# Recurrences of an RWKV-7 layer: solving a batch ahead of need, with a copy of the keys reloaded when it is turned

## The chip, the cores and the metric

One core of one Trainium2 chip runs the whole program in one launch. The metric is device microseconds of that core, as the median of several executions; lower is better. A core has five engines that each work through their own instructions in order and meet through semaphores: PE (matmuls and transposes by matmul; its weight loads are shown as PEld), DVE, ACT and POOL (elementwise work), and SP, which issues the DMAs.

## The reference, cut to what matters

Two layers of a backbone over 1024 latent and 256 context tokens, width 1024, in float32. Layer 0 is attention with a gated recurrence and an expert mixture. Layer 1, where the change lies, is a bidirectional RWKV-7 mixing followed by an expert mixture. For each of 16 heads of 64 channels, in both directions, the mixing runs this recurrence over the context and then over the latent tokens:

```python
def step(s, inp):
    w_t, k_t, v_t, a_t, b_t = inp[:5]
    sa = jnp.einsum('bhvk,bhk->bhv', s, a_t)
    s = s * w_t[:, :, None, :] + sa[..., None] * b_t[:, :, None, :] + v_t[..., None] * k_t[:, :, None, :]
    y = jnp.einsum('bhvk,bhk->bhv', s, inp[5]) if r is not None else None
    return s, y
```

Afterwards the outputs of both directions are added, normalised by head, given a bonus, gated and multiplied by an output matrix (`rw_wo`), and the expert mixture and a final norm follow.

## The kernel before

The program runs in stages: layer 0, the projections of layer 1 (`Proj1`, which writes the images of queries, keys and values to DRAM as `iAR`, `iBK`, `iV`), the recurrences (`Wkv.run`, here 2296 to 2938 us of the profile), the output projection (`mix_out1`, 2825 to 3028 us, overlapping the end of the recurrences) and the experts of layer 1 (`moe`, from 3035 us).

The recurrence is cut in chunks of 64 tokens (`C`). A chunk is one step of matmuls with a state of 64x64 for each head, once the inverse of a unit triangular 64x64 matrix of that chunk is known. A *group* holds one chunk of four heads-and-directions on each half of the 128 partitions. There are 4 sets of heads (`pg`) and 20 chunks, so 80 groups and 80 steps. Eight groups make a *batch*; there are 10 batches, and their inverses are computed together, since each has 32 matrices. In the order of steps two sets of heads alternate, so that one set's state update has about one step of slack.

What happens to a group, with the names of the code:
- `images` loads keys (`bk`, one load for two groups: L1941 to L1943) and queries (`ar`, L1952), multiplies them (PE, into tile `G`, L1960), copies the triangles into the batch's tile `lab` (ACT, L1962 and L1964) and masks the rest (DVE, L1970).
- `turn` transposes the group's keys (PE, tile `T`, L1980) and copies them to `bkt` (ACT, L1981).
- `solve` has two parts. The first transposes `lab` into `lp` (DVE, L2010), clears `rp` (POOL) and does 31 rounds of a multiply and a subtract (L2018 and L2019), on DVE for the first batch and on POOL for all later ones. The second transposes `rp` back into `db` and `dtb` (DVE, L2022 and L2023) and copies a quarter of it (ACT, L2026). `db` is the same memory as `lp`.
- `join`, called for each half of a batch, builds the 64x64 inverses out of two 32x32 ones by matmuls (L2039 and L2047) and ACT copies (L2042 and L2049). It reads `db`.
- `values` loads and turns the values of two groups (tile `vt`, L1990; PE L1993; ACT L1999 and L2000).
- `step` multiplies query images with the state (`XS`, L2064; ACT copy `xs`, L2066), then by the inverse (L2072, ACT L2074), gives the new state (L2078; DVE `st`, L2084 and L2086; ACT L2089) and the output (`Y`, L2069 and L2094; ACT `ys`, L2099; a store at L2109).

`run` prepares 16 groups and the first batch's inverses, and then issues the steps. Step `at` (from 0) also turns the group 15 ahead, makes the images 16 ahead, and, at fixed places of a batch, runs the parts of `solve` and `join` for the *next* batch: the first part of `solve` in the batch's step 0 (`at % 8 == 0`), after the last `join` of the running batch has read `db`; the second part in step 6, between the step's first matmuls and its multiplication by the inverse; `join` from step 7 to step 1 of the next batch.

On PE, ACT and DVE the instructions of the steps are issued in the order in which the code emits them (`manual_schedule`). That ends with step 66 (`FREE`); the rest, and the order on SP and POOL everywhere, is a planner's. Memory comes from rings: `NG` = 17 places for `ar` (five of them in memory named `early`, which the projections held before), `bkt` and `lrb`, two for `lab`, four pairs of groups for `bk` (`bks`, in `early`).

The output projection takes over the memory of the recurrences (class `Tail`): its weights `raws[0..3]` are loaded into `bs`, `bks[0]`, `bks[1]`, `bks[2]`, and the row that scales them (`row0`, L818) into `bks[3]`. Its first half treats the heads of the first two sets, tile by tile of 128 tokens, 8 tiles (product at L853); its second half the other heads (L902).

Of the kernel before, what the change touches and what calls it, by code (L numbers as in the profile page):

```python
# [1322 lines left out]
C = 64  # L1323
# [556 lines left out]
class Wkv:  # L1880
# [3 lines left out]
    NG = 17  # L1884
# [8 lines left out]
    def __init__(self, g, p, pp):  # L1893
        nc, A = g.nc, g.A
        self.g, self.p, self.pp = g, p, pp
        self.iAR = [g.dram(f"iAR{k}", [128, 20, 4, 2 * C]) for k in range(4)]
        self.iBK = [g.dram(f"iBK{k}", [128, 20, 4, 2 * C]) for k in range(4)]
        self.iV = [g.dram(f"iV{k}", [128, 10, 4, 2 * C]) for k in range(4)]
        self.mask = g.wmask
        self.ring = {}  # L1900
        self.st = {}
        self.at = {}

        a, b = (g.wkvp.tile([128, 5, 1024], F, name="early", tag=n) for n in ("mvh", "mvl"))
        self.bks, self.bs, self.ars = [a[:, k] for k in range(4)], a[:, 4], [b[:, k] for k in range(5)]
        self.nar = self.nbk = 0
        self.persist("dtb", [128, 32, C], 2)
# [14 lines left out]
    def new_batch(self, groups):  # L1922

        lab = self.p.tile([128, 32, C], F, name="lab", tag="lab", bufs=2)
        if len(groups) < 8:
            self.g.nc.gpsimd.memset(lab[:, 16:, :], 0.0)
        return dict(groups=groups, lab=lab, gr=[])

    def images(self, b):
# [6 lines left out]
        if k == 0:  # L1936
            b["bk"] = bk = self.bks[self.nbk % 4].rearrange("p (c u x) -> p c u x", c=2, u=4)
            self.nbk += 1
            src = self.iBK[pg][:, c:c + 2].rearrange("p c u t -> p (c u) t")
            dst = bk.rearrange("p c u t -> p (c u) t")  # L1940
            nc.sync.dma_start(dst[0:64], src[0:64])  # L1941
            nc.sync.dma_start(dst[64:128, :, C:], src[64:128, :, 0:C])
            nc.sync.dma_start(dst[64:128, :, 0:C], src[64:128, :, C:])  # L1943
# [27 lines left out]
        b["gr"].append(dict(pg=pg, c=c, ar=ar, lrb=lrb, lu=4 * n, bk=bk))  # L1971

    def turn(self, gr):

        g, nc, p, pp = self.g, self.g.nc, self.p, self.pp
        gr["bkt"] = bkt = p.tile([128, 4, 2 * C], F, name="bkt", tag="bkt", bufs=self.NG)
        tp = pp.tile([128, 4, 128], F, name="T", tag="T", bufs=self.NT)
        bk = gr.pop("bk")
        for u in range(4):
            nc.tensor.transpose(tp[:, u], bk[:, u], g.ident)  # L1980
        nc.scalar.copy(bkt, tp)  # L1981
# [20 lines left out]
    def solve(self, b, eng):  # L2002
# [18 lines left out]
        db = lp  # L2021
# [89 lines left out]
    def run(self):  # L2111
# [7 lines left out]
        made, turned, ys = 0, 0, {}  # L2119
# [10 lines left out]
        def turn():  # L2130
            nonlocal turned
            if turned < N:
                self.turn(bs[turned // 8]["gr"][turned % 8])
                turned += 1
# [5 lines left out]
        def pair():  # L2140
            for _ in range(2):
                images()
            turn()
            turn()
# [14 lines left out]
        while made < 16:  # L2159
            pair()  # L2160
        none = iter(())
        solve, joins, last = none, [none, none], none
        E = mybir.EngineType
        with ExitStack() as written:
            written.enter_context(g.tc.manual_schedule(engines={E.PE, E.Activation, E.DVE}))
            for at, (k, n) in enumerate(order):
# [17 lines left out]
                if at:  # L2184
                    turn()
                if at % 8 == 6:
                    run(solve)
# [12 lines left out]
                if at % 8 == 0:  # L2200
                    run(joins[1])
                    if more:
                        solve = self.solve(bs[k + 1], g.nc.gpsimd)
                        run(solve)
                images()
# [5 lines left out]
class Tail:  # L2211


    def __init__(self, w):
# [5 lines left out]

        def half(n, dt=R, tag="bkt", bufs=w.NG):
            return sum((get(tag, bufs, dt, 512) for _ in range(n)), [])
# [11 lines left out]
        a = halves(get("lab", 2, F, m=2)) + half(4, F) + halves(ar(3, F) + b[:1])  # L2234
        cs = half(4)
        mw = halves(get("lab", 2, R, m=2) + get("lp", 1, R) + get("rp", 1, R)) + half(4) + halves(ar(2, R))
# [149 lines left out]
```

## Time and profile before

| | us |
|---|---|
| median of 3 runs (3696.99 to 3702.59) | 3699.67 |
| the profiled execution | 3699.94 |
| its span, first to last instruction | 3698.2 |
| granted TensorE clock, mean of the span | 0.92 |

Over the span PE is busy for 3168.2 us (86%), DVE 2475.2 (67%), ACT 2199.7 (59%), POOL 1083.1 (29%). These shares are averages over stages with different limits; the change touches one stage of some 640 us and what follows it.

### The profile page before, as it was taken

The page shows a single profiled execution, that of the slowest core. Times are in us where ns is not written, and L with a number is a line of the kernel's source. Part 1 is how long each engine was busy: PE and PEld are TensorE (multiplying, and loading weights), DVE is VectorE, ACT ScalarE, POOL GpSimd, SP SyncE. Part 2 cuts the span into 40 slices and gives each one's busy share as a digit, 9 for nine tenths or more (in the row PEclk, how much of TensorE's full clock was granted, in tenths as well). Part 3 has the DMA queues.
Part 4 walks back from the last instruction along what each step waited for, and adds up shares of the span by engine and source line. Part 5 has one row for each costly group of instructions (what it writes and reads, how often), then busy time and mean ns, then how long its engine had stood idle before and what let it go on. Part 6 is the DMA issues. An engine that isn't in the chain of part 4 may idle for free. (4 is left out here: it accounts for less than half of the span.)

```text
span 3698.2 us, 68014 instructions
## 1 busy us (share of the span) xinstructions
PE 3168.2 (86%) x27017; PEld 2487.3 (67%) x27017; DVE 2475.2 (67%) x3341; ACT 2199.7 (59%) x3985; POOL 1083.1 (29%) x1195
## 2 busy tenths in 40 slices
PE   7997989599999999798888876676767876999998
PEld 5884677477777777567766765565655554887776
DVE  5666783666766766666985895433445457888888
ACT  4564573366666666335644663676666544878776
POOL 2213002301111111234653661555466221111111
PEclk9998999799999999898889987888788987999999
DMA  5117716468888887444862783343336559999995
GB/s 200 59 39 273 282 34 202 165 248 285 280 290 290 280 286 272 152 129 130 220 186 67 197 222 95 103 101 97 89 110 183 155 200 321 384 377 384 354 379 216
DMA packets 579366, 770.59 MB, mean 208 GB/s; under 512 B 106868, under 2 KB 371048, under 8 KB 572904
## 3 DMA queue, kind: packets, MB, share of 16 engines
q1 hardware_dynamic: 564104, 717.22, 57.8%
q0 software_dynamic: 14944, 49.03, 4.8%
q8 instruction: 212, 3.47, 0.4%
q14 instruction: 106, 0.87, 0.1%
HBM read 638.96 MB, written 127.18 MB: 207 GB/s over the span
## 5 line engine op out<-in xcount | busy, mean ns | idle before, releaser
L192 DVE TENSOR_TENSOR elo<-raw,ehi 128x2048 fp32r<-128x2048 f32 x378 | 859.4, 2289 | 296.6 <-ACT ehi L191 295.4
L191 ACT ACTIVATE ehi<-raw 128x2048 fp32r<-128x2048 f32 x384 | 734.9, 1916 | 214.0 <-PE h L1158 82.4
L1158 PE MATMUL h<-ehi,xhi 128*128 128x512 f32 x512 | 208.0, 406 | 0.0
L1158 PE MATMUL h<-elo,xhi 128*128 128x512 f32 x512 | 203.0, 396 | 0.0
L1158 PE MATMUL h<-ehi,xlo 128*128 128x512 f32 x512 | 202.8, 396 | 0.0
L2018 POOL TENSOR_TENSOR tmp<-lp,rp 128x31 f32<-128x31 f32 (+15 forms) x279 | 145.0, 520 | 169.6 <-DVE lp L2010 148.8
L1102 PE MATMUL h<-ehi,wx 128*128 128x512 f32 x512 | 163.3, 396 | 0.0
L2019 POOL TENSOR_TENSOR rp<-rp,tmp 128x31 f32<-128x31 f32 (+15 forms) x279 | 153.8, 551 | 21.5
L1477 PE MATMUL pj<-mvh,whi 128*128 128x384 f32 (+1 forms) x512 | 149.3, 326 | 2.6 <-ACT vv L1787 2.5
L1477 PE MATMUL pj<-mvl,whi 128*128 128x256 f32 (+1 forms) x512 | 146.5, 320 | 4.1 <-DVE mvl L192 3.8
L1477 PE MATMUL pj<-mvh,wlo 128*128 128x256 f32 (+1 forms) x512 | 148.6, 323 | 0.7 <-POOL wlo L192 0.7
L1122 POOL DMA_INDIRECT xg<-s_hl,idx x16 | 15.8, 987 | 451.1 <-PE tr L1137 446.7
L1265 PE MATMUL y<-ehi,wh 128*128 128x512 f32 x512 | 143.6, 397 | 2.3 <-DVE wh L192 2.3
L1970 DVE TENSOR_TENSOR ar<-G,wmask 64x512 f32<-64x512 f32 (+1 forms) x110 | 69.9, 635 | 112.5 <-PE G L1960 103.1
L2078 PE MATMUL XS<-sv,bkt 128*64 128x64 f32 x1216 | 59.4, 247 | 94.4 <-ACT sv L2074 93.5
L1080 ACT ACTIVATE xm<-tr,c_mcol 128x128 f32<-128x128 f32 x256 | 95.6, 453 | 60.9 <-PE tr L1069 36.5
L1087 POOL DMA_INDIRECT xg<-s_hl,idx x16 | 24.2, 1511 | 362.5 <-PE tr L1069 339.1
L2078 PEld LDWEIGHTS XS<-sv,bkt 128*64 128x64 f32 x1216 | 48.0, 154 | 109.5 <-ACT sv L2074 99.2
L1226 POOL DMA_INDIRECT s_xl<-ys,idx x16 | 52.4, 3274 | 230.7 <-DVE ys L1225 230.7
L216 PE MATMUL pj<-xhi,whi 128*128 128x512 f32 (+1 forms) x336 | 119.1, 355 | 0.0
L216 PE MATMUL pj<-xlo,whi 128*128 128x512 f32 (+1 forms) x336 | 119.0, 354 | 0.0
L216 PE MATMUL pj<-xhi,wlo 128*128 128x512 f32 (+1 forms) x336 | 118.8, 354 | 0.0
(562 smaller groups left out, 9328.0 us busy)
## 6 DMA issues: line engine op xcount, KB each, us to landing
raw<-in_exp_w SPq DMA_DIRECT2D x379, 1024.0 KB
modw<-in_mod_w SPq DMA_DIRECT2D x48, 1024.0 KB
wraw<-in_rw_rkv SPq DMA_DIRECT2D x48, 512.0 KB
s_iAR<-ar SPq DMA_DIRECT2D x32, 384.0 KB
s_iBK<-bk SPq DMA_DIRECT2D x32, 384.0 KB
ar<-s_iAR SPq DMA_DIRECT2D x88, 128.0 KB
early<-s_iBK SPq DMA_DIRECT2D x40, 256.0 KB
early<-s_iBK SPq DMA_DIRECT2D x80, 128.0 KB
```

The source lines that it names most:

```text
L191: nc.scalar.activation(hi, src, AF.Copy)
L192: (sub or nc.vector).tensor_tensor(lo, src, hi.bitcast(F), op=ALU.subtract)
L216: nc.tensor.matmul(ps[:m, :b - a], wt[:, k, :m], xt[:, k, a:b], start=k == 0 and n == 0, stop=k == kt - 1 and n == 2)
L1080: self.nc.scalar.activation(f[:, k], src[:, k], AF.Identity, scale=a, bias=b)
L1102: nc.tensor.matmul(hs[which], a[:, kk], b[:, k], start=kk == 0 and a is x[0] and b is w[1], stop=kk == 7 and a is x[1])
L1158: nc.tensor.matmul(hs[which], a[:, kk], b[:, k], start=kk == 0 and a is x[0] and b is w[1], stop=kk == 7 and a is x[1])
L1265: nc.tensor.matmul(y[:, 512 * n:512 * n + 512], a[:, kk % 4], b[:, k, 512 * n:512 * n + 512], start=kk == 0 and a is hh and b is hi, stop= ...
L1477: nc.tensor.matmul(ps[q], wk[:, k], xk[:, a:b], start=k == 0 and n == 0, stop=k == KT - 1 and n == 2)
L1970: nc.vector.tensor_tensor(o4, g4, self.mask[r, None, :, x].to_broadcast([r.stop - r.start, 2, 2, x.stop - x.start]), op=ALU.mult)
L2018: eng.tensor_tensor(t, lp[:, k + 1:, k:k + 1].to_broadcast([128, n, w]), rp[:, k:k + 1, 0:w].to_broadcast([128, n, w]), op=ALU.mult)
L2019: eng.tensor_tensor(rp[:, k + 1:, 0:w], rp[:, k + 1:, 0:w], t, op=ALU.subtract)
L2078: nc.tensor.matmul(S[R[h], u], bkt[:, u, V[h]], sv[:, u, V[h]], start=True, stop=True)
```

## The change

- The inverses of a batch are begun one batch earlier. `solve` for the second batch starts before step 0; in step 5 of each batch the second part of `solve` for the next batch is run, and right behind it the first part for the batch after that. Before, the two parts of one solve lay in step 0 and step 6 of the same batch.
- For this, `db` gets memory of its own (`bs`) instead of `lp`'s, `lab` has three places instead of two, and images are made 18 groups ahead (`LEAD`) with `NG` = 20 places for `ar` and `lrb`.
- Keys are turned two steps ahead instead of 15, and `bkt` has 5 places instead of 17. Since `bk` is not kept until then, `turn` loads the group's keys a second time, by three DMAs of its own (`load_bk`). Of the four places of `bks`, two now serve the images (a pair of groups each) and two the turns (four groups in all).
- `Tail`, which reuses the memory, takes half-size tiles from `ar` instead of `bkt`, and `lab` in threes.

```diff
--- before.py
+++ after.py
@@ -1881,7 +1881,8 @@
 
 
 
-    NG = 17
+    NG = 20
+    LEAD = 18
     NYS = 2
     NSV = 5
     NT = 2
@@ -1903,7 +1904,7 @@
 
         a, b = (g.wkvp.tile([128, 5, 1024], F, name="early", tag=n) for n in ("mvh", "mvl"))
         self.bks, self.bs, self.ars = [a[:, k] for k in range(4)], a[:, 4], [b[:, k] for k in range(5)]
-        self.nar = self.nbk = 0
+        self.nar = self.nbk = self.nbt = 0
         self.persist("dtb", [128, 32, C], 2)
 
     def persist(self, name, shape, n):
@@ -1921,10 +1922,17 @@
 
     def new_batch(self, groups):
 
-        lab = self.p.tile([128, 32, C], F, name="lab", tag="lab", bufs=2)
+        lab = self.p.tile([128, 32, C], F, name="lab", tag="lab", bufs=3)
         if len(groups) < 8:
             self.g.nc.gpsimd.memset(lab[:, 16:, :], 0.0)
         return dict(groups=groups, lab=lab, gr=[])
+
+    def load_bk(self, dst, src):
+
+        nc = self.g.nc
+        nc.sync.dma_start(dst[0:64], src[0:64])
+        nc.sync.dma_start(dst[64:128, :, C:], src[64:128, :, 0:C])
+        nc.sync.dma_start(dst[64:128, :, 0:C], src[64:128, :, C:])
 
     def images(self, b):
 
@@ -1934,13 +1942,9 @@
         ctxt = c < 4
         w = C if ctxt else 2 * C
         if k == 0:
-            b["bk"] = bk = self.bks[self.nbk % 4].rearrange("p (c u x) -> p c u x", c=2, u=4)
+            b["bk"] = bk = self.bks[self.nbk % 2].rearrange("p (c u x) -> p c u x", c=2, u=4)
             self.nbk += 1
-            src = self.iBK[pg][:, c:c + 2].rearrange("p c u t -> p (c u) t")
-            dst = bk.rearrange("p c u t -> p (c u) t")
-            nc.sync.dma_start(dst[0:64], src[0:64])
-            nc.sync.dma_start(dst[64:128, :, C:], src[64:128, :, 0:C])
-            nc.sync.dma_start(dst[64:128, :, 0:C], src[64:128, :, C:])
+            self.load_bk(bk.rearrange("p c u t -> p (c u) t"), self.iBK[pg][:, c:c + 2].rearrange("p c u t -> p (c u) t"))
         bk = b["bk"][:, k]
         if self.nar % self.NG < 5:
             ar = self.ars[self.nar % self.NG].rearrange("p (u x) -> p u x", u=4)
@@ -1968,14 +1972,16 @@
         for out, src, r, x in parts:
             o4, g4 = (t.rearrange("p (i d) t -> p i d t", d=2) for t in (out, src))
             nc.vector.tensor_tensor(o4, g4, self.mask[r, None, :, x].to_broadcast([r.stop - r.start, 2, 2, x.stop - x.start]), op=ALU.mult)
-        b["gr"].append(dict(pg=pg, c=c, ar=ar, lrb=lrb, lu=4 * n, bk=bk))
+        b["gr"].append(dict(pg=pg, c=c, ar=ar, lrb=lrb, lu=4 * n))
 
     def turn(self, gr):
 
         g, nc, p, pp = self.g, self.g.nc, self.p, self.pp
-        gr["bkt"] = bkt = p.tile([128, 4, 2 * C], F, name="bkt", tag="bkt", bufs=self.NG)
+        bk = self.bks[2 + self.nbt % 4 // 2].rearrange("p (c u x) -> p c u x", c=2, u=4)[:, self.nbt % 2]
+        self.nbt += 1
+        self.load_bk(bk, self.iBK[gr["pg"]][:, gr["c"]])
+        gr["bkt"] = bkt = p.tile([128, 4, 2 * C], F, name="bkt", tag="bkt", bufs=5)
         tp = pp.tile([128, 4, 128], F, name="T", tag="T", bufs=self.NT)
-        bk = gr.pop("bk")
         for u in range(4):
             nc.tensor.transpose(tp[:, u], bk[:, u], g.ident)
         nc.scalar.copy(bkt, tp)
@@ -2018,7 +2024,7 @@
             eng.tensor_tensor(t, lp[:, k + 1:, k:k + 1].to_broadcast([128, n, w]), rp[:, k:k + 1, 0:w].to_broadcast([128, n, w]), op=ALU.mult)
             eng.tensor_tensor(rp[:, k + 1:, 0:w], rp[:, k + 1:, 0:w], t, op=ALU.subtract)
         yield
-        db = lp
+        db = self.bs.rearrange("p (u t) -> p u t", t=32)
         nc.vector.transpose(db.rearrange("p u s -> p s u"), rp.rearrange("p t s -> p s t"))
         nc.vector.transpose(dtb[:, :, 32:].rearrange("p u t -> p t u"), rp)
         for h in range(2):
@@ -2116,7 +2122,7 @@
         bs = [self.new_batch(b) for b in plan[:2]]
         order = [(k, n + m) for k in range(NB) for n in (0, 4) for m in (0, 2, 1, 3)]
         N = len(order)
-        made, turned, ys = 0, 0, {}
+        made, ys = 0, {}
 
         def images():
             nonlocal made
@@ -2127,11 +2133,10 @@
             self.images(bs[made // 8])
             made += 1
 
-        def turn():
-            nonlocal turned
-            if turned < N:
-                self.turn(bs[turned // 8]["gr"][turned % 8])
-                turned += 1
+        def turn(at):
+            if at < N:
+                k, n = order[at]
+                self.turn(bs[k]["gr"][n])
 
         def values(at):
             k, n = order[at]
@@ -2140,8 +2145,6 @@
         def pair():
             for _ in range(2):
                 images()
-            turn()
-            turn()
 
         def run(it, n=1):
             for _ in range(n):
@@ -2156,10 +2159,14 @@
             run(self.join(bs[0], half), 9)
         values(0)
         values(1)
-        while made < 16:
+        for at in range(2):
+            turn(at)
+        while made < self.LEAD:
             pair()
         none = iter(())
-        solve, joins, last = none, [none, none], none
+        joins, last = [none, none], none
+        solve = self.solve(bs[1], g.nc.gpsimd)
+        run(solve)
         E = mybir.EngineType
         with ExitStack() as written:
             written.enter_context(g.tc.manual_schedule(engines={E.PE, E.Activation, E.DVE}))
@@ -2181,10 +2188,7 @@
                 run(last)
                 run(step)
 
-                if at:
-                    turn()
-                if at % 8 == 6:
-                    run(solve)
+                turn(at + 2)
                 if at % 8 == 0:
                     run(joins[0])
                 if at % 8 == 1:
@@ -2199,10 +2203,13 @@
                     run(joins[0])
                 if at % 8 == 0:
                     run(joins[1])
-                    if more:
-                        solve = self.solve(bs[k + 1], g.nc.gpsimd)
+                images()
+                if at % 8 == 5:
+                    run(solve)
+
+                    if k + 2 < NB:
+                        solve = self.solve(bs[k + 2], g.nc.gpsimd)
                         run(solve)
-                images()
                 if at % 4 >= 2 and at + 2 < N:
                     values(at + 2)
             run(last, 9)
@@ -2218,8 +2225,8 @@
             t = pool.tile([128, m, n], dt, name="tail", tag=tag, bufs=bufs)
             return [t[:, k] for k in range(m)]
 
-        def half(n, dt=R, tag="bkt", bufs=w.NG):
-            return sum((get(tag, bufs, dt, 512) for _ in range(n)), [])
+        def half(n, dt=R):
+            return halves(ar(n // 2, dt))
 
         def ar(n, dt):
             return sum((get("ar", w.NG - 5, dt) for _ in range(n)), [])
@@ -2231,9 +2238,9 @@
         d = [w.ring["dtb"][(w.at["dtb"] + k) % 2].rearrange("p (k a) b -> p k (a b)", k=2)[:, j] for k in range(2) for j in range(2)]
         raw = [w.bs] + w.bks[:3] + b[1:]
         ax = ar(2, F)
-        a = halves(get("lab", 2, F, m=2)) + half(4, F) + halves(ar(3, F) + b[:1])
+        a = halves(get("lab", 3, F, m=2)) + half(4, F) + halves(ar(3, F) + b[:1])
         cs = half(4)
-        mw = halves(get("lab", 2, R, m=2) + get("lp", 1, R) + get("rp", 1, R)) + half(4) + halves(ar(2, R))
+        mw = halves(get("lab", 3, R, m=2) + get("lp", 1, R) + get("rp", 1, R)) + half(4) + halves(ar(2, R))
         cs += halves(ar(1, R))
         hT = halves(raw[3:4] + ar(1, F))
         small = [get("lrb", w.NG, F, 256)[0] for _ in range(4)]
```

## Rows read from the trace of the kernel before

**Rows 1.** Chain of waits, 2393 to 2771 us, its shares by line.
```profile
by line: POOL rp L2019 27.4%; POOL tmp L2018 25.9%; issue 9.6%; PE T L2039 3.7%; DVE lp L2022 3.2%; DVE lp L2010 3.2%; DVE dtb L2023 2.8%; PE XS L2072 2.8%; ACT dtb L2026 2.0%; PE T L2047 2.0%; ACT sv L2000 1.8%; ACT sv L1999 1.7%; ACT sv L
```

**Rows 2.** Busy time by stretch: stretch, length, PE, PEld, DVE, ACT, POOL, clock, DMA share, GB/s.
```profile
2393.75:2770.32 376.57, 265.81 (x6912) 230.26 (x6912) 150.64 (x248) 246.71 (x624) 203.35 (x384) 0.83 0.38 97
2787.86:2913.68 125.82, 98.78 (x1601) 70.23 (x1603) 64.93 (x110) 73.63 (x281) 67.20 (x83) 0.87 0.56 166
2913.68:2959.80 46.12, 39.09 (x288) 21.12 (x284) 23.50 (x55) 18.64 (x104) 14.19 (x12) 0.99 0.68 208
3200.00:3400.00 200.00, 198.56 (x891) 160.02 (x891) 176.52 (x106) 158.14 (x142) 25.16 (x11) 1.00 1.04 379
```

**Rows 3.** Waits, 2330 to 2771 us: who waited for whom, total us, times, longest.
```profile
PE XS L2078 <- ACT sv L2074: 77.6, 8, 15.6
DVE lp L2022 <- POOL rp L2019: 77.5, 8, 12.0
DVE lp L2010 <- PE T L2039: 31.3, 6, 6.2
PE G L1960 <- DMA early<-s_iAR: 8.2, 6, 2.1
...
PE T L1993 <- DMA vt<-s_iV: 1.7, 3, 0.9
```

**Rows 4.** Timeline of one cycle: start, duration, engine, line, [idle before, releaser].
```profile
2393.75 2.00 DVE L2022 STREAM_TRANSPOSE lp<-rp 128x1024 f32<-128x1024 f32 x1 [11.64 <-POOL rp L2019]
...
2397.54 2.10 ACT L2026 COPY dtb<-dtb 32x1024 f32<-32x1024 f32 x2 [14.67 <-DVE dtb L2023]
...
2404.03 0.37 ACT L2066 COPY xs<-XS 128x256 f32<-128x256 f32 x1
...
2411.32 0.37 ACT L2066 COPY xs<-XS 128x256 f32<-128x256 f32 x1
...
2416.14 2.00 DVE L2010 STREAM_TRANSPOSE lp<-lab 128x1024 f32<-128x1024 f32 x1 [4.92 <-PE T L2039]
...
2418.29 0.25 POOL L2018 TENSOR_TENSOR tmp<-lp,rp 128x31 f32<-128x31 f32 x1 [19.50 <-DVE lp L2010]
...
2418.70 0.37 ACT L2066 COPY xs<-XS 128x256 f32<-128x256 f32 x1
...
2424.47 0.37 ACT L2066 COPY xs<-XS 128x256 f32<-128x256 f32 x1
...
2432.32 0.37 ACT L2066 COPY xs<-XS 128x256 f32<-128x256 f32 x1
...
2437.86 0.37 ACT L2066 COPY xs<-XS 128x256 f32<-128x256 f32 x1
...
2441.86 0.37 ACT L2066 COPY xs<-XS 128x256 f32<-128x256 f32 x1
...
2445.95 0.37 ACT L2066 COPY xs<-XS 128x256 f32<-128x256 f32 x1
...
2456.12 2.01 DVE L2022 STREAM_TRANSPOSE lp<-rp 128x1024 f32<-128x1024 f32 x1 [9.74 <-POOL rp L2019]
...
2466.41 0.37 ACT L2066 COPY xs<-XS 128x256 f32<-128x256 f32 x1
```

**Rows 5.** SP's issue of a key load: ns min/median/max, 2330 to 2770 us.
```profile
L1942 SPq DMA_DIRECT2D early<-s_iBK x26: 589/597/1645, 2330.3 to 2727.0; - x26
```

**Rows 6.** DMA queue, 2330 to 2770 us: packets, MB, share of 16 engines.
```profile
q1 hardware_dynamic: 77090, 42.47, 37.3%
```

**Rows 7.** Waits, 2200 to 2945 us; these three lie before step 0.
```profile
PE T L1980 <- DMA early<-s_iBK: 14.1, 3, 6.5
```

**Rows 8.** The output projection's products: ns min/median/max, first and last start.
```profile
L853 PE MATMUL G<-early,tail x96: 592/592/1119, 2825.7 to 2947.7; 128*128 128x512 f32 x96
L853 PE MATMUL G<-early x32: 592/592/697, 2896.3 to 2957.6; 128*128 128x512 f32 x32
L902 PE MATMUL G<-tail x168: 387/393/776, 2959.8 to 3024.6; 128*128 128x512 f32 x168
```

## The prediction

> **What bounds the kernel now.** I read the chain of waits of the recurrence stage first. Over half of it is POOL's 31 rounds of the solve, L2018 and L2019 [rows 1], though POOL is busy for only 203 of 377 us there, less than ACT (247) and PE (266) [rows 2]. So the stage waits for a latency, not for a full engine. The waits show where: DVE stands at L2022 until POOL's last round, 77.5 us in 8 waits [rows 3], about 10 us in a full cycle, and since all engines are in order, ACT (behind L2026) and then PE (up to 15.6 us at a time) stand too.
>
> The timeline gives the cycle. From L2022 to L2022 it takes 376.57 us for six cycles, 62.8 us for 8 steps [rows 2]. The copies `xs` mark the steps 15 to 23 [rows 4]; step 16 opens a batch, and the L2022 at 2393.75 lies in step 14. Their distances are 7.3, 7.4, 5.8, 7.9, 5.5, 4.0, 4.1 and 20.5 us. The last contains the stop for POOL. A step without `values` takes 4.0 and one with it 5.5; those next to a batch's start are longer by their joins. POOL itself is idle from the end of one solve until L2010 of the next, because `lp` is read as `db` by the joins (19.5 us before its first round; L2010 waited 4.9 us for L2039) [rows 4].
>
> **The change, part by part.**
>
> *The solve moves a batch ahead.* L2022 is reached in step 5, a cycle after POOL began, instead of six steps after. POOL's own loop is L2010 to L2022, 39.98 us, plus L2022 and L2023 until ACT's copies start, 3.8 us [rows 4]: 43.8 us. If the steps need longer than that, the wait for POOL is gone: −9.7 us for this cycle. What stays is the second part itself: DVE's two transposes, 3.8 us, and ACT's two copies, 2.1 us [rows 4]. They now stand behind the images of step 5 and ahead of step 6's `xs`. DVE's masks of that image still run then, for which I add 0.5 us, an estimate; step 5 grows by 0.5 + 3.8 + 2.1 = 6.4 us, and step 6 loses its stop. L2010's further 2 us on DVE follow L2023; behind them stand the state updates L2084 and L2086, which ACT needs only after L2026 and the next three copies, so I cost it at nothing (2 us a cycle if that cover is gone).
>
> *The new cycle.* Steps 7 and 0 as they are (7.3 + 7.4); step 1 5.8; step 2 5.6, since its 7.9 has 2.3 us of waiting for queries, whose places (20 for 18 ahead, before 17 for 16) now come free a step earlier [rows 3, 4]; then 5.5, 4.0, 4.1 + 6.4 and 5.5. Sum 51.6 us, above POOL's 43.8. Bounds: below, ACT cannot do better than its 246.7/6 = 41.1 us of work [rows 2] plus the 6.4 us in which it waits or copies for the solve, of which 2.1 are in the 41.1 already: 45.4. Above, PE's clock may still fall in the shorter stop and DVE's 2 us may show: 55.6. I take 51.6, for which every term is a measured step. Saving 62.8 − 51.6 = 11.2 us a cycle; seven cycles (batches 1 to 7) give 78 us (51 to 122). In batch 0 POOL starts no later and the steps there have a smaller stop: −2.
>
> *Keys loaded twice.* Three DMAs more in each step. An SP issue takes 0.6 us [rows 5]; by my count of the code a cycle had 40 issues (16 queries, 12 keys, 8 outputs, 4 values), 24 us, and gets 64, 38 us of 51.6. SP stays under full, but it also waits in order. The packets: 77090 took 37.3% of 16 engines in 440 us, 34 ns each [rows 6]. A step adds 64 of 2 KB and 512 of 256 bytes; 8 x 576 x 34 ns / 16 = 9.8 us a cycle on top of 0.38 x 62.8 = 23.9 [rows 2]: 33.7 of 51.6 us, 65% busy. The second loads have four places and so up to four steps (20 us) of lead; nobody waits for them as long as SP issues them early. No row shows such a load in the steps. Nearest are the values' loads, 1.7 us of waiting in seven cycles [rows 3], or 0 to 2 us for all; far off, the key loads before step 0, where a transpose stood 4.7 us on average [rows 7]. I take 0, as the steps' own loads are nearest.
>
> The Trainium skill (DMA: Bandwidth & Descriptors, Specifications) asks for pieces of at least 512 bytes for line rate. The trace agrees: this stage moved 97 GB/s at a share of 0.38, that is 255 at a full share, where the experts' long pieces gave 379 at 1.04 [rows 2]. If a 256-byte piece costs what 512 bytes would, the second loads come to an estimated 12 us a cycle and the share to 70%, still not a bound.
>
> *Before step 0.* 14 turns and a prefetch of the output weights (`bs` is no longer free) leave, two more images come, and keys have two places instead of four. The three waits above, 14.1 us [rows 7], are what could go (−14) or, with fewer places, double for two pairs (+9). I take 0.
>
> *The end.* At step 64 the sum so far is −80. From there to the output projection's second half the kernel before took 2787.9 to 2959.8, 172 us [rows 2, 8], with POOL's last solve and most of the first half's products between the steps. Now the last solve is done early and without the projection's work on POOL, but the products start later: `row0` sits in `bks[3]`, which the last turn frees in step 77. So: 13 steps to there. Without images I estimate 4.6 us each, from the 4.0 and 5.5 above, 60; the joins and the last solve 12; rows of four tiles prepared between, a guess of 10: 82 us, against the 125.8 from step 64 to step 77 before. Then the stretch that took 46.1 us and held half the products [rows 2, 8] must hold all: 64 products more at 0.59 us, 38 us. 82 + 46 + 38 = 166, −6. Bounds: +38 if the steps stay as slow as they were (125.8 + 46 + 38 = 210), −35 if the products slip between the steps after all. Behind that, the experts load at a full DMA share [rows 2], and start when the projection ends, so all gained before is kept.
>
> **Sum** against the execution's 3699.9: −2 − 78 + 0 + 0 − 6 = −86, **3614 us**; the median of the runs shown differs from that execution by 0.3 us.
>
> **The rivals.**
> 1. *The steps become slower than their old selves* (SP at three quarters, DMA at two thirds, the clock): 55.6 us a cycle or somewhat more. For it speaks that SP waits in order, behind places freed by PE; against it that waits for loads were small. −2 − 50 − 6: 3642, up to 3660.
> 2. *The end gives back*: the products pile up behind step 77 while the planner's order keeps the last steps slow. −80 + 38: 3658. For it, `row0`'s late place is certain.
> 3. *More is won*: the cycle falls towards 45.4 us and the products overlap: −2 − 122 − 6 and less, 3570 or under. Against it, every step would have to beat its old self.
> 4. *Slower than before*: the second key loads are on the path. If the planner places them on SP in the step that needs them, PE stands at L1980 in each of 80 steps, with U and everything after it behind. At 4.7 us [rows 7] that is +376, near 3990 us. It decides from 86/80 = 1.1 us a step on. Against it, four places and loads of the same queue that are early.
> 5. *The wait for POOL does not go away*, because `lab` of the batch two ahead is complete only in the very step that starts its solve. A step's delay of L2010 still leaves 43.8 + 6 = 50 us against 51.6, so this costs at most a few us and belongs to rival 1.
>
> **How the numbers follow.** Forecast (3575 to 3642) 0.54; rival 1 (3642 to 3660) 0.14 and rival 2 about as far (to 3668, or both together to 3692) 0.13; rival 3 0.10; no change 0.02; rival 4 0.07. What a measurement can tell from no change here is 0.2%, about 7 us. Range 3568 to 3668: it leaves out most of rival 4, no change, the worst of rivals 1 and 2 together and the best of rival 3, near 2 in 10. The likeliest case alone: 3575 to 3642. Faster (forecast, rivals 1 to 3) 0.91, same 0.02, slower (rival 4) 0.07.
>
> **What would show it.** Right: L2022 no longer waits for POOL except perhaps in the first batch; L2022 to L2022 near 52 us; the distance of `xs` from step 5 to 6 near 10.5 and from 6 to 7 near 5.5; POOL's idle time ahead of L2010 a few us, DMA share near 0.65 in the stage, step 64 some 80 us earlier. L853's first product later against the steps, around step 77. Wrong: waits at L1980 for `s_iBK` in most steps; SP issues back to back; steps 1 to 4 longer than 5.8, 5.6, 5.5, 4.0; or a gain at step 64 that is smaller by the second half's first product. I am least sure of the end, where the order is a planner's.

## The result and the profile after

The changed kernel takes 3652.19 us, median of 4 runs (3644.67 to 3659.86), against 3698.33 us for the kernel before (4 runs, 3689.40 to 3702.59): a ratio of 0.9878, 95% interval 0.9849 to 0.9908. That is 46 us faster where 86 were forecast; the median lies 38 us above the forecast time and inside its range. The profiled executions differ by 55.3 us (3699.94 and 3644.67); the readings below are of these two.

The gain has to be read at two places. The `xs` copy of step 64 (ACT's copy of that step's first products) starts at 2715.56 us instead of 2787.86 [rows 2], 72.3 us earlier (forecast: 80). The first product of the projection's second half, L902, starts at 2906.8 instead of 2959.8 [rows 8], only 53 us earlier. So the end gave back 19 us, where the forecast had it gain 6.

In the recurrence the chain of waits, 2327 to 2696 us, no longer holds POOL's rounds, which had 53% of it [rows 1]:

```profile
by line: PE XS L2078 8.9%; PE G L1964 8.8%; ACT sv L2095 5.0%; PE XS L2084 4.3%; ACT sv L2080 4.3%; PE T L2053 4.2%; DVE early L2028 4.2%; issue 4.0%; PE T L1986 3.7%; ACT dtb L2032 3.4%; DVE dtb L2029 3.4%; PE XS L2070 3.3%; PE Y L2100 3.2
```

The waits of that stretch (seven cycles; total us, times, longest) have turned round: POOL now stands for DVE's back transposes, 12.3 us a cycle, and ACT stands 4 us a cycle for them.

```profile
POOL rp L2018 <- DVE dtb L2029: 86.0, 7, 13.6
...
PE XS L2078 <- ACT xs L2072: 53.2, 22, 6.4
...
ACT dtb L2032 <- DVE dtb L2029: 28.1, 7, 4.2
DVE ar L1974 <- DMA early<-s_iBK: 20.4, 6, 3.9
```

By the line of the first back transpose (ns min/median/max, first and last start) a cycle is (2695.4 − 2327.1) / 7 = 52.6 us, against 62.8:

```profile
L2028 DVE STREAM_TRANSPOSE early<-rp x8: 1969/1995/2078, 2327.1 to 2695.4; 128x1024 f32<-128x1024 f32 x8
```

The timeline of steps 21 to 23 (DVE's lines, then ACT's) shows what is left of the stop, to be read beside [rows 4]:

```profile
2426.94 1.39 DVE L1974 TENSOR_TENSOR ar<-G,wmask 64x512 f32<-64x512 f32 x2 [2.86 <-PE G L1964]
...
2428.39 0.37 ACT L2072 COPY xs<-XS 128x256 f32<-128x256 f32 x1
...
2432.83 2.00 DVE L2028 STREAM_TRANSPOSE early<-rp 128x1024 f32<-128x1024 f32 x1
2434.68 1.91 DVE L2029 STREAM_TRANSPOSE dtb<-rp 128x1024 f32<-128x1024 f32 x1
2436.39 1.90 DVE L2016 STREAM_TRANSPOSE lp<-lab 128x1024 f32<-128x1024 f32 x1
2438.17 0.43 DVE L2090 TENSOR_TENSOR st<-XS,st 128x256 f32<-128x256 f32 x1
...
2436.62 2.10 ACT L2032 COPY dtb<-dtb 32x1024 f32<-32x1024 f32 x2 [4.16 <-DVE dtb L2029]
2438.74 0.37 ACT L2072 COPY xs<-XS 128x256 f32<-128x256 f32 x1
...
2444.70 0.37 ACT L2072 COPY xs<-XS 128x256 f32<-128x256 f32 x1
```

L2028 carries no wait for POOL. From step 5 of the batch to step 6 (21 to 22) it takes 10.3 us, of which 4.16 are ACT's wait for DVE and 2.10 its copies; from step 6 to 7 it takes 6.0.

At the end, two stops stand out. Timeline of ACT and of DVE, steps 65 and 66, then 77 and 78:

```profile
2722.96 0.37 ACT L2072 COPY xs<-XS 128x256 f32<-128x256 f32 x1 [0.69 <-PE XS L2070]
...
2742.59 0.26 ACT L599 ACTIVATE tail<-tail 128x64 f32<-128x64 f32 x1 [10.67 <-POOL rp L2025]
...
2744.64 0.37 ACT L2072 COPY xs<-XS 128x256 f32<-128x256 f32 x1
...
2741.03 0.69 DVE L596 TENSOR_REDUCE tail<-tail 128x8 f32<-128x512 f32 x1 [17.77 <-POOL tail L593]
2741.82 0.69 DVE L597 SCALAR_TENSOR_TENSOR tail<-tail 128x512 f32<-128x512 f32 x1
...
2813.65 0.38 ACT L2072 COPY xs<-XS 128x256 f32<-128x256 f32 x1
...
2835.81 0.35 ACT L2072 COPY xs<-XS 128x256 f32<-128x256 f32 x1
...
2820.04 3.41 DVE L824 TENSOR_TENSOR early<-early 128x1024 f32<-128x1024 f32 x1 [4.05 <-issue]
2823.37 2.56 DVE L2092 TENSOR_TENSOR st<-st,gC 128x256 f32<-128x256 f32 x1
2825.85 8.87 DVE L824 TENSOR_TENSOR early<-early 128x1024 f32<-128x1024 f32 x3
2834.65 0.41 DVE L2090 TENSOR_TENSOR st<-XS,st 128x256 f32<-128x256 f32 x1
```

From 65 to 66 (21.7 us) DVE waits at the row sum L596 for an addition on POOL, L593, which POOL reaches only at 2739.74, behind 27 of the last solve's 31 rounds. Two queues stand behind it: on DVE the state update L2090, and on ACT the row's squares L599, which need DVE's L597 and come ahead of the `xs` copy of step 66 in ACT's order. The products that this copy reads were done at 2731.4. From 77 to 78 (22.2 us) the gate row, whose load (L818) is issued only at 2814.7, is multiplied into the weights on DVE (L824) among the state updates, and ACT stands 8.5 us for the state update L2092.

The first of these stops is not new. ACT's timeline of the kernel before, steps 65 and 66, 24.3 us apart with the same row work between them:

```profile
2794.83 0.37 ACT L2066 COPY xs<-XS 128x256 f32<-128x256 f32 x1 [0.56 <-PE XS L2064]
...
2804.44 0.26 ACT L599 ACTIVATE tail<-tail 128x64 f32<-128x64 f32 x1 [9.23 <-DVE tail L597]
...
2819.10 0.37 ACT L2066 COPY xs<-XS 128x256 f32<-128x256 f32 x1
```

### The profile page after: what moved, and what is told of

The parts are those of the page before. It is cut to its first block, busy times and chain, and to the rows that moved or that the text cites. A ratio compares the mean times of both kernels' runs of the same rounds, so it can differ in the third digit from the quotient of the medians.

```text
span 3642.9 us, 68486 instructions
## 1 busy us (share of the span) xinstructions
PE 3172.0 (87%) x27017; PEld 2489.2 (68%) x27017; DVE 2484.0 (68%) x3341; ACT 2199.5 (60%) x3985; POOL 1084.3 (30%) x1195
## 5 line engine op out<-in xcount | busy, mean ns | idle before, releaser
L1974 DVE TENSOR_TENSOR ar<-G,wmask 64x512 f32<-64x512 f32 (+1 forms) x120 | 79.5, 662 | 168.4 <-PE G L1964 140.9
L2078 PE MATMUL XS<-xs,dtb 64*64 64x64 f32 x1280 | 65.1, 244 | 77.4 <-ACT xs L2072 69.9
L1087 POOL DMA_INDIRECT xg<-s_hl,idx x16 | 24.2, 1513 | 361.6 <-PE tr L1069 338.6
L1165 PE MATMUL hc<-raw,xc 128*32 128x256 f32 x2048 | 117.1, 381 | 0.0
```

Source lines behind the costliest of these rows:

```text
L1165: nc.tensor.matmul(hc[32 * q:32 * q + 32, :256], xcs[e][:, kk], raws[kk // 4, q // 2][:, kk % 4, 256 * (q % 2):256 * (q % 2) + 256], start ...
L2078: nc.tensor.matmul(U[R[h], u], dtb[R[h], gr["lu"] + u], xs[R[h], u], start=True, stop=True)
```

## The experiments

Eleven runs: the changed kernel once more, and ten edits of it. Code is cut to the lines that matter (`...`). Of each I read three numbers: the cycle (from the first and last L2028, as above), the start of `xs` in step 64, and the distance from there to the first L902, called the end. In the first profile of the changed kernel these are 52.6, 2715.6 and 191.2 us; before, the end was 171.9.

**The control (e5).** No edit.

> The changed kernel once more, unaltered, beside the others of this group, to see what two executions of it differ by. In its first profile some opening steps of a batch ran at a granted clock of 1.00 and took 7.4 us, others at 0.62 and took 9.1. Theory (which of them fall is chance): another pattern of 7.4 and 9 to 10 us, a cycle between 52.6 and 54.5 us, and 3645 to 3660 us. Rival (the pattern belongs to the kernel): the same batches fall, a cycle of 52.6 us.

3659.95 us (ratio 0.9905, 0.9889 to 0.9922).

```profile
L2028 DVE STREAM_TRANSPOSE early<-rp x8: 1945/1994/2096, 2329.7 to 2706.5; 128x1024 f32<-128x1024 f32 x8
```

A cycle of 53.8 us, step 64 at 2727.9, the end 192.0. So two executions of one kernel differ by 12 us up to step 64, and hardly in the end. Which opening steps of a batch were slow changed (7.4 us in one, 8.4 to 9.7 in the six others), as the theory had it. Differences under 10 us decide nothing below.

**The old places of the solve (e1).** It is begun in step 0 of the batch before and ended in step 6.

```
-        solve = self.solve(bs[1], g.nc.gpsimd)
-        run(solve)
...
+                if at % 8 == 6:
+                    run(solve)
...
                 if at % 8 == 0:
                     run(joins[1])
+                    if more:
+                        solve = self.solve(bs[k + 1], g.nc.gpsimd)
+                        run(solve)
                 images()
-                if at % 8 == 5:
-                    run(solve)
-
-                    if k + 2 < NB:
-                        solve = self.solve(bs[k + 2], g.nc.gpsimd)
-                        run(solve)
```

> The changed kernel (18 groups ahead, keys loaded twice, blocks of three, inverses with a place of their own) with one part undone: the solve is begun at step 0 of the batch before and ended at step 6, as in the kernel before. Theory (the whole gain is the wait for POOL at the back transposes, which starting a batch ahead takes away): DVE waits for POOL about 10 us a cycle again, the distance from one first back transpose to the next goes from 52.6 back to 61 to 63 us, and the time to about 3690 to 3720 us. Rival (the blocks, the place of the inverses and the lead of 18 save time by themselves, POOL beginning earlier because its block is no longer read by the joins): a cycle of 55 to 58 us and 3665 to 3680 us.

3676.55 us (0.9942, 0.9925 to 0.9959): about half of the gain stays. The cycle is (2732.4 − 2392.3) / 6 = 56.7 us, the rival's. Waits of these six cycles, and one batch of the timeline:

```profile
DVE early L2028 <- POOL rp L2025: 28.5, 6, 6.9
```

```profile
2409.05 1.93 DVE L2016 STREAM_TRANSPOSE lp<-lab 128x1024 f32<-128x1024 f32 x1
...
2409.43 0.37 ACT L2072 COPY xs<-XS 128x256 f32<-128x256 f32 x1
...
2444.78 0.37 ACT L2072 COPY xs<-XS 128x256 f32<-128x256 f32 x1
...
2448.92 2.01 DVE L2028 STREAM_TRANSPOSE early<-rp 128x1024 f32<-128x1024 f32 x1 [3.71 <-POOL rp L2025]
...
2459.20 0.37 ACT L2072 COPY xs<-XS 128x256 f32<-128x256 f32 x1
```

L2016 opens the solve 0.4 us ahead of the batch's first `xs`, where before it came 4.8 us after it, behind the joins [rows 4]. The stop falls from 20.5 to 14.4 us and the wait for POOL from 10 to under 5. So of the 10.2 us saved in a cycle 6.1 belong to what this kernel keeps (the inverses' own place, the lead, the places for queries; which of them was not tried), and 4.1 to the start a batch ahead, or 2.9 against the control's cycle.

**The late copies (e4).** ACT's two copies go to the end of step 6.

```
         nc.vector.transpose(dtb[:, :, 32:].rearrange("p u t -> p t u"), rp)
+        b["db"] = db
+        yield
         for h in range(2):
...
                     run(solve)
-
+                    copies = solve
...
                     values(at + 2)
+                if at % 8 == 6:
+                    run(copies)
```

> The changed kernel with ACT's two copies behind the back transposes moved from the end of step 5 to the end of step 6. Theory (of the longer step 5, 10.3 us against 4, the part of 4.2 us is ACT waiting for DVE's two transposes, in front of the next step's copies): the wait goes, a cycle falls from 52.6 to 48 to 49 us, and the time by 25 to 32 us, to about 3622 us. Rival (step 5 is long because DVE itself is taken: the transposes of 3.8 us stand ahead of the state updates and images that the next step needs): the wait moves to the state's copy or to the images, the cycle stays at 51 to 53 us and the time within 10 us.

3661.2 us (0.9901, 0.9884 to 0.9918), the control's time, as the rival had it. From step 5 to 6 it takes 4.1 us, but from 6 to 7 12.5, and the cycle (2717.4 − 2327.9) / 7 = 55.6. The timeline of ACT shows the wait at its new place, the state's copy, because the state updates stand behind the three transposes:

```profile
2445.54 0.83 ACT L2096 COPY sv<-st 64x256 f32<-64x256 f32 x2 [4.79 <-DVE st L2093]
```

**The parted transposes (e7).** One goes ahead of the images of step 5, two ahead of those of step 6, where DVE waits for PE in any case (2.86 us at L1974 in the timeline of the changed kernel), and the copies behind them.

```
         nc.vector.transpose(db.rearrange("p u s -> p s u"), rp.rearrange("p t s -> p s t"))
+        b["db"] = db
+        yield
         nc.vector.transpose(dtb[:, :, 32:].rearrange("p u t -> p t u"), rp)
+        yield
...
-                images()
                 if at % 8 == 5:
                     run(solve)
-
+                if at % 8 == 6:
+                    back = solve
+                    run(back)
                     if k + 2 < NB:
                         solve = self.solve(bs[k + 2], g.nc.gpsimd)
                         run(solve)
+                images()
+                if at % 8 == 6:
+                    run(back)
```

> The changed kernel with the solve's three transposes on DVE parted: the first back transpose ahead of the images of step 5, the second and the transpose that begins the next solve ahead of the images of step 6, where DVE waits for PE's products anyway, and ACT's two copies at the end of step 6. Theory (what stayed of the stop is three transposes in a row on DVE, 5.8 us, with either ACT's copies or the state updates behind them, and after the stop a granted clock of 0.5 for some 5 us and again in step 0): the distance from step 5 to 6 falls from 10.3 to 4 to 5 us, step 6 to 7 grows to 7 to 9, step 0 takes 7.4 in all batches, the cycle falls to 47 to 49 us and the time by 25 to 40 us against the control. Rival (DVE or ACT is short of time in steps 5 to 7 in any order, as in the run with the late copies): the cycle stays above 51 us and the time within 10 us.

3625.5 us (0.9807, 0.9792 to 0.9823), 34 us under the control. The `xs` copies of steps 21 to 24:

```profile
2423.01 0.37 ACT L2074 COPY xs<-XS 128x256 f32<-128x256 f32 x1
2427.10 0.37 ACT L2074 COPY xs<-XS 128x256 f32<-128x256 f32 x1
2434.82 0.37 ACT L2074 COPY xs<-XS 128x256 f32<-128x256 f32 x1
2443.09 0.37 ACT L2074 COPY xs<-XS 128x256 f32<-128x256 f32 x1 [0.44 <-PE XS L2072]
```

Steps 5 and 6 take 4.1 and 7.7 us, as expected. The cycle falls to (2680.8 − 2324.4) / 7 = 50.9 us only, between the theory's 47 to 49 and the rival's 51: step 7 grows to 8.3, and the opening steps stay at 8 to 10. Steps 5 to 7 take 20.1 us together, against 23.1 in the changed kernel. Step 64 comes at 2700.5, 27.4 us before the control's. So the row of three transposes on DVE was part of what remained of the stop, 3 us a cycle; the late copies (e4) had only moved the wait.

**The keys, doubled and left out (e6, e9).**

```
-        self.load_bk(bk, self.iBK[gr["pg"]][:, gr["c"]])
+        for _ in range(2):                        # e6
+            self.load_bk(bk, self.iBK[gr["pg"]][:, gr["c"]])
...
-        self.load_bk(bk, self.iBK[gr["pg"]][:, gr["c"]])
+        if self.nbt <= 4:                         # e9
+            nc.gpsimd.memset(bk, 0.0)
```

> The changed kernel with each late key load issued twice in a row into the same place: three DMAs more per step, nothing else. Theory (SP and the DMA queues have room; the second key loads cost nothing): the DMA share of the stage goes from 0.65 to about 0.85, the cycle stays within 1 us and the time within 10 us of the control. Rival (the loads are near the bound, on SP or on the queues, and already cost something): the cycle grows by 3 us or more, waits for s_iBK show at L1986, and the time by over 25 us.

3820.85 us (1.0333, 1.0316 to 1.035), 161 us above the control: the size is beyond the rival's, the place another. The waits of seven cycles, (2859.3 − 2348.7) / 7 = 72.9 us each, SP's queue last:

```profile
PE T L2000 <- DMA vt<-s_iV: 107.7, 14, 11.8
...
SPq L1933 <- DMA early<-s_iBK: 69.0, 54, 3.3
```

SP's queue waits for the landing of the first copy before it issues the second into the same place, a wait that the edit itself brought. The values' loads, behind it in SP's order, come late, and PE stands for them. DMA is not full: its share in these cycles is 0.58, that of the changed kernel 0.65. So the run shows what an SP that is kept waiting costs, and not what the second loads cost; hence e9.

> The changed kernel without the second key loads: the two places from which the keys are turned are set to zero once and turned again and again, so the three DMAs of each late load are left out (the state's products then use zero keys, and the output isn't the reference's). Theory (the second loads cost nothing, term 0 of the prediction): the same cycle, 52.6 to 54 us, and a time within 10 us of the control's 3660. Rival (SP, 41 us busy and standing for places in the rest, is as near the bound in the changed kernel as the doubled loads made it): the cycle falls by 3 us or more and the time by over 25 us.

3652.98 us (0.9881, 0.9865 to 0.9898), 7 us under the control, and a cycle of (2703.4 − 2327.5) / 7 = 53.7 against 53.8. The stretch of these cycles (length, busy times, clock, DMA share, GB/s):

```profile
2327.50:2703.40 375.90, 306.69 (x8048) 268.95 (x8048) 177.07 (x293) 286.79 (x727) 240.17 (x450) 0.88 0.47 118
```

The share falls from 0.65 to 0.47 and the cycle does not move: the second loads cost the steps nothing. DVE's waits for keys fall from 20.4 us in the changed kernel to 3.8 here, so those waits were not on the path either. The granted clock is 0.88 here and 0.89 in the control, so PE ran no differently on zero keys. In DMA time the second loads are 0.65 x 52.6 − 0.47 x 53.7 = 9 us a cycle.

**Other places for the end (e2).**

```
-        raw = [w.bs] + w.bks[:3] + b[1:]
+        raw = b[1:] + [w.bs] + w.bks[1:]
...
-        a = halves(get("lab", 3, F, m=2)) + half(4, F) + halves(ar(3, F) + b[:1])
+        a = halves(get("lab", 3, F, m=2)) + half(4, F) + halves(ar(3, F) + w.bks[:1])
...
-            ... "row0": w.bks[3:], ...
+            ... "row0": b[:1], ...
```

> The changed kernel with other places for the output projection's data: the gate row and the raw weights go where keys' images and the inverses of the last batch lay, free by about step 65, and no longer where the last keys are turned, free at step 77. Theory A (the late places hold up the stretch from step 77 to 78, 22.2 us, because the rows are multiplied by the gate on DVE in front of the state updates): that distance falls to 4 to 8 us, the projection's products start some 15 us earlier, and the time falls by 12 to 20 us, to about 3634 us. Rival (the end is held by the order in which POOL and DVE prepare rows, behind the last solve): the 21.7 us between steps 65 and 66 stay, what is won at step 77 is lost in later products, and the time stays within 5 us of 3652.

3623.11 us (0.98, 0.9783 to 0.9818), 29 us under the changed kernel's median above and 37 under the control's, though its cycle was 54.1 us. The row's load and the products:

```profile
L818 SPq DMA_DIRECT2D early<-s_m x1: 382/382/382, 2700.4 to 2700.4; - x1
```

```profile
L853 PE MATMUL G<-early,tail x96: 592/592/1219, 2732.7 to 2876.8; 128*128 128x512 f32 x96
...
L902 PE MATMUL G<-tail x168: 387/389/500, 2885.7 to 2948.6; 128*128 128x512 f32 x168
```

The row comes 114 us earlier and the first product 91. The end takes 2885.7 − 2731.6 = 154.1 us, 37 less. But not as theory A had it: the step from 77 to 78 still takes 16.7 us, and steps 64 to 77 take 106.4 us against 98.1. The stop has moved one step ahead, to 64 to 65 (16.1 us), where PE waits at a product for a weight that POOL multiplies between the last solve's rounds:

```profile
2744.51 2.07 PE L853 MATMUL G<-early,tail 128*128 128x512 f32 x2 [6.03 <-POOL early L824]
```

What went is the pile of products behind the steps: from step 77 to L902 47.7 us instead of 93.2.

**The rows' sum on DVE (e3).**

```
-        nc.gpsimd.tensor_tensor(y, y, z, op=ALU.add)
+        nc.vector.tensor_tensor(y, y, z, op=ALU.add)
```

> The changed kernel with one instruction moved: the sum of two row tiles ahead of the head norm goes from POOL to DVE, so that DVE no longer waits for POOL at the end of its last solve. Theory B (the 21.7 us between steps 65 and 66 are DVE standing at the row sum of squares behind POOL, with the state updates behind it): that distance falls to 6 to 9 us, DVE gets 16 x 1.3 us at most of work, and the time falls by 8 to 15 us, to about 3640 us. Rival (what is won there is waited for again at step 77, since the gate row comes then whatever the steps do): step 77 comes earlier by as much and the row with it, or the distance from 77 to 78 grows and the time stays within 5 us.

3663.45 us (0.9908, 0.9882 to 0.9933): no gain. DVE first stood 7.44 us at the moved sum itself, and then for POOL at the last solve's own back transpose, which the planner had now put there:

```profile
2745.99 0.78 DVE L593 TENSOR_TENSOR tail<-tail 128x512 f32<-128x512 f32 x1 [7.44 <-PE Y L2100]
...
2756.66 2.01 DVE L2028 STREAM_TRANSPOSE early<-rp 128x1024 f32<-128x1024 f32 x1 [8.25 <-POOL rp L2025]
```

Steps 65 to 67 take 12.6 + 15.4 us instead of 21.7 + 6.8. The sum starts 15.6 us after step 64, where POOL's started 24.2 after it in the changed kernel: its place among POOL's rounds was worth some 9 us of the stop, and they were lost again at L2028. Theory B's gain did not come: moving the sum moves the wait.

**Both gains together (e8, e10, e11).** e8 is e7 with the places of e2. The other two are e8 with one edit more: e10 keeps the written order until step 72 (`FREE = 72`), and e11 puts the second four weights elsewhere (`raw = b[1:] + w.bks[:2] + [w.bs] + w.bks[2:3]`, the rows' last pair in `w.bks[3:]`).

> The parted transposes together with the early places of the gate row and the raw weights. Theory (the two gains lie in different stretches, before step 64 and after it, and the experts start as much earlier): the sum of both, 3585 to 3600 us, and step 64 to the end of the projection's products 150 to 155 us as with the places alone. Rival (with shorter cycles the data of the end comes no sooner, since it depends on loads and on rows written by the steps): no more than 10 us better than the places alone, 3613 us or above.

> Parted transposes and early places, and the written order of PE, ACT and DVE is kept until step 72 instead of 66, so that no row of the projection stands ahead of the last solve's transposes or the state updates until then. Theory (the stop of 19.6 us between steps 65 and 66 is the tail's rows standing ahead of the steps in DVE's and ACT's order): the stop goes, step 72 comes some 15 us earlier, and the time falls by 8 to 15 us to about 3613. Rival (the products set the end: what they lose between the steps they need behind them): step 72 is earlier and the products' end is not; 3620 to 3635 us.

> Parted transposes and early places, with the second four weights in the places of the images' keys, of the inverses and of one pair of late keys, and a pair of the rows' tiles in the last late place. Theory (POOL stood 41.5 us at a product of the gate row and a late weight, with the rows' sums behind it, and that is why the two gains did not add): the wait falls under 15 us, the products end 15 to 25 us earlier, and the time is about 3600 us. Rival (the wait is only one of several behind the steps' own data): the time stays within 8 us of 3625.

3624.73 us (0.98, 0.9784 to 0.9816), 3634.49 (0.9837, 0.9818 to 0.9855) and 3620.13 (0.9792, 0.9776 to 0.9809). None adds the two gains. e8 reaches step 64 at 2709.4, 22 us before e2, and then needs 186.4 us for the end. Stretches from step 64 to L902, of e2 and of e11:

```profile
2731.60:2885.70 154.10, 138.03 (x1930) 92.32 (x1931) 74.65 (x143) 91.28 (x346) 55.84 (x66) 0.94 0.69 194
```

```profile
2710.20:2893.00 182.80, 144.68 (x1930) 97.52 (x1931) 77.73 (x154) 96.89 (x385) 65.96 (x75) 0.87 0.61 173
```

With as many products and transposes, PE idles 16 us in e2 and 38 in e11. In e8 POOL stood 41.5 us at one weight that had not landed; with e11's places that wait is 27.2, for a turn, and the time falls by less than can be told apart. The stop from 65 to 66 is there in e8 and in e11 (19.6 and 23.3 us), and holding the written order to step 72 (e10) did not remove it (22.0): in all three DVE stands 13 to 18 us at L596 for L593. Which order of POOL's and DVE's work would keep both gains was not found.

## Why the prediction was partly right

*The bound and its removal.* Right in the recurrence: the wait for POOL at the back transposes is gone, L2022's 77.5 us [rows 3]. But e1 shows that the reason was only half seen. The forecast gave the 9.7 us to the start a batch ahead. Freeing `lp` from the joins, adding places and lead took 6.1 us of a cycle alone, and the batch ahead 4.1. One sign was missed: POOL's idle time ahead of its next solve was to be "a few us" and is 12.3 a cycle, where the forecast's own numbers, a cycle of 51.6 and 40.0 from L2010 to L2022, leave 11.6.

*The new cycle.* Forecast 51.6, measured 52.6, in the control 53.8. The steps themselves came nearly as summed: 7.4, 6.0, 5.6, 5.5, 4.0, 10.3, 6.0 and 6.8 in batch 2, together 51.6, though step 7 was 0.5 shorter and step 6 0.5 longer than summed. The mean is longer because the opening step took 8.5 to 9.6 us in four of the other six; in all four the granted clock was 0.62 to 0.80, in the three of 7.4 us it was 1.00. That is rival 1's clock, at 1 to 2 us a cycle: by the `xs` copies, steps 8 to 64 took 68.8 us less than before, where 78 were forecast. In the control, where six opening steps were slow, step 64 came only 60.0 us earlier than before, of a forecast 80.

*DVE's further 2 us.* Costed at nothing, since ACT needs the state only after its copies. Right where it was placed, and e4 shows the condition: with the copies gone from there, ACT waits 4.79 us for the state. Parting the three transposes (e7) still gave 3 us a cycle.

*Keys loaded twice.* The cost of 0 holds (e9), the DMA share was met (0.65), and rival 4 did not come. The forecast's 34 ns a packet gave 9.8 us of DMA time a cycle for the second loads; by e9 it is 9. The share that the forecast estimated beside it, 70% if a piece of 256 bytes costs what 512 would, is too high for the measured 65; the 512 bytes are those of the Trainium skill (DMA: Bandwidth & Descriptors, Specifications). The margin on SP was thinner than told: in e6, where SP waits for landings, a cycle is 19 us longer.

*Before step 0, and batch 0.* Forecast 0 and −2; step 0 came at 2295.5 instead of 2297.7 us, and steps 0 to 8 took 49.8 instead of 51.2.

*The end.* This is the step that failed, and by mechanism, not by size alone: "82 + 46 + 38 = 166, −6" was 191. The thirteen steps took 98.1 us instead of 82, for a stop of 21.7 us that the sum did not have. With that step at some 5 us the thirteen would have taken 98.1 − 16.7 = 81.4. The forecast had the last solve done early and a guess of 10 us for the rows; the last solve ran on POOL until 2744.6, 29 us past step 64, with the rows' sum between its rounds, and the kernel before had already stood 24.3 us at the same place. The 84 us behind them were 93.2, with the 22.2 of the late row in them. That is rival 2 at half its price of 38, which had 13 in 100: products behind step 77, last steps held by the planner's order. e2 shows that the products' late start came with the places. The stop from 65 to 66 is read from the trace; no run took it away without another in its stead, and its cause is shown only as far as e3 and e10 go.

Put together, by the `xs` copies and the first L902: −2.2 − 1.3 − 68.8 + 19.3 = −53.0; the remaining 2.3 of the 55.3 us between the profiled executions lie behind L902.

The measured 3652 lies outside the forecast's own stretch (3575 to 3642), in what was left to rivals 1 and 2, and both came in part. That it is inside the range is owed to the room left for them.

## What to carry to other kernels

When a wait on a slow helper engine goes, look for what else was serial at that place: here three 2 us transposes in one row on DVE, worth another 27 to 34 us (3625.5 against 3652 and 3660 of the changed kernel's two measurements) once they were put where DVE waits anyway. A buffer shared between one solve and the next is a wait too; a place of its own, with more lead and places, gave at least as much as starting earlier. And where stages overlap, a data place that is freed late moves the whole next stage: follow each tile of that stage to the last reader of its place before adding up times, and look in the profile of before for stops that the sum of plain steps would leave out.

## What was not expected of the hardware

The opening step of a batch took 7.4 us at one granted clock of PE and 9.1 at another. Stretches of the changed kernel: the stop of step 13, the start of step 14, and two opening steps (length, PE busy time, ..., clock, DMA share, GB/s):

```profile
2380.40:2386.10 5.70, 0.18 (x2) 0.00 (x0) 5.67 (x5) 2.08 (x2) 1.36 (x3) 0.88 0.65 169
2386.10:2390.00 3.90, 3.45 (x64) 3.28 (x64) 0.34 (x1) 2.78 (x8) 3.23 (x9) 0.50 1.05 193
...
2399.90:2407.30 7.40, 6.41 (x240) 5.80 (x240) 1.42 (x3) 5.98 (x15) 6.62 (x11) 1.00 0.74 193
2604.70:2613.80 9.10, 8.29 (x216) 7.48 (x218) 1.66 (x4) 5.56 (x13) 8.16 (x13) 0.62 0.46 106
```

After a stop in which PE worked 0.18 of 5.7 us, the next 3.9 us ran at 0.50, the lower level, 1.2 GHz. One of the two opening steps ran wholly at the upper level, 2.4 GHz, the other mostly at the lower. Over the seven opening steps of each of the two executions, all four at 1.00 took 7.4 us, the three at 0.80 took 8.5 to 8.7, and the seven at 0.62 to 0.70 took 9.1 to 9.7. Which batches were hit differed between the executions.

A multiplication of 128x1024 on DVE had a median of 3.37 us in the changed kernel, where POOL did the same kind of multiplication in the same 12 us, and 1.23 in e2, where most had no such neighbour; POOL's own went from 2.93 to 2.35 (lines of the changed kernel, then of e2). The Trainium skill (SBUF — State Buffer, Who interferes with whom) says that a DVE instruction with two inputs in SBUF contends with a GpSimd (POOL) instruction that reads SBUF, and that this is an exclusive lock. The trace agrees: 1.23 + 2.35 us, one behind the other, would be 3.58, near DVE's 3.37.

```profile
L824 POOL TENSOR_TENSOR early<-early x4: 2340/2927/3332, 2820.0 to 2828.1; 128x1024 f32<-128x1024 f32 x4
L824 DVE TENSOR_TENSOR early<-early x4: 2287/3370/3408, 2820.0 to 2832.4; 128x1024 f32<-128x1024 f32 x4
```

```profile
L824 POOL TENSOR_TENSOR early<-early x4: 2341/2353/2362, 2711.7 to 2838.0; 128x1024 f32<-128x1024 f32 x4
L824 DVE TENSOR_TENSOR early<-early x4: 1224/1226/1548, 2717.3 to 2826.0; 128x1024 f32<-128x1024 f32 x4
```
